# A hybrid decoder block: projections in another order, a top-k over 50 pairs, rows normed in steps, loads issued elsewhere

## The chip, the cores and the metric

The kernel runs on one core of a Trainium2 chip, whose engines work in parallel, each through its own queue in order: TensorE (PE in the profile; PEld is its weight load), VectorE (DVE), ScalarE (ACT), GpSimd (POOL) and SyncE (SP), which only starts transfers. ACT's and POOL's queues start transfers too. The metric is the device time of one execution in microseconds (us).

## What is computed

One decoder block over 528 tokens (16 meta tokens and 512) of 2048 channels: an RMS norm, one wide projection, a convolution module and a gated linear attention (GLA) side by side, their gated sum projected back, and then a channel mixer (PEER) in which each token picks experts by a product key.

```python
proj = rmsnorm(h, norm1_g) @ w_in        # split into a_conv, q, k, v, r, a_low, g_merge
y_conv = conv_module(a_conv)             # h*sigmoid, 31 taps, layer norm, silu, @ w_conv_out
y_gla = gla(q, k, v, r, a_low)           # chunked, rms norm, * silu(r), @ w_gla_out
gates = sigmoid(g_merge)
h = h + (gates[:, :D] * y_conv + gates[:, D:] * y_gla) @ w_out
xn = rmsnorm(h, norm2_g); q = xn @ peer_wq           # 8 heads of 2 x 128
s1 = q[..., :128] @ k1; s2 = q[..., 128:] @ k2       # 128 keys each
v1, i1 = top_k(s1, 16); v2, i2 = top_k(s2, 16)
cand = v1[:, None] + v2[None, :]                     # 16 x 16 pairs
top_s, pos = top_k(cand, 16); idx = i1[pos//16]*128 + i2[pos%16]
w = softmax(top_s) * gelu(U[idx] @ xn)               # 16384 experts
out = rmsnorm(h + w @ V[idx], normf_g)[16:]
```

## The kernel before

Activations stand with channels on the 128 partitions and tokens along the row. Each fp32 product is made of three matmuls over a number split into a high and a low part (x = xh + xl, weights whi + wlo: xl by whi, xh by whi, xh by wlo), 48 matmuls for 16 tiles of 128 channels. `_weights` (line 59) loads a weight tile in two halves through SP's queue, ACT casts each half to `whi` (L69), and DVE or POOL subtracts to `wlo` (L72): `g.lopool` names the halves that POOL takes. `whi` and `wlo` have three buffers each, so one and a half projections can be prepared ahead. Loop order is written by hand; a list scheduler with a cost model of its own then sets the order on each engine from it, and `high_priority` and `issue_after` shift its choice.

The stages: `_norm1`; `_phase_a` with 16 convolution tiles, each two projections of 528 columns (`_conv`) and after it one of the 48 gate projections of 512 columns (`_gates`, which stores sigmoid or silu rows to `rgd`), then the GLA heads with four gate projections, then the other 28 gate projections, under which the convolution's layer norm statistics and normed rows (`_conv_stats`, `_conv_norm`) are made; `_mixers_out`, first `wco` (convolution) and then `wgo` (GLA, whose rows o*r are made at its start); `_residual`; `_select`, 16 projections `wq` with `_scores` (a top-16 of 128 scores, four blocks of tokens) and after each second one `_head_select` (top-16 of 256 pairs, two `_pick`s of the indices), and beside them `_dense_row`, which norms the rows that the experts' matmuls read (`dh`, `dl`).

The 160 gathered tokens (of 512) get their experts' rows by indirect DMA (`rows`) and DVE; the 352 dense ones get a matmul with all 16384 experts: 128 up tiles `_up_tile` (`pu`, gelu rows `gel`, the first 64 stored to `hlag`) and 16 groups of down products (`_down_quarter`, `pv`). The first `NPRE` up tiles run while DVE still selects; their `wlo` are POOL's. `_w_piece` multiplies four gelu rows by the gate matrix `gt` and splits them (`wh`, `wl`). In the last group `_Final` adds the residual `hx` to the sums `yT` before each quarter and finishes the gathered tokens.

Of the kernel before, what the change touches and what calls it, by code (L numbers as in the profile page):

```python
# [6 lines left out]
F32 = mybir.dt.float32  # L7
# [22 lines left out]
EPS = 1e-6  # L30
TB0 = 128
# [9 lines left out]
NINT = 16  # L41
NPRE = 8
# [83 lines left out]
def _norm1(g, sp):  # L126
# [3 lines left out]
    with g.tc.tile_pool(name="n1", bufs=1, side="right") as tp:  # L130
        ss = [tp.tile([P, L], F32, name="ss", bufs=2) for _ in range(2)]
        xe = []
        with g.tc.high_priority(offset=100000):
            for c in range(KT // 2):
                xe.append(tp.tile([P, 2, L], F32, name="xe", bufs=8))
                nc.sync.dma_start(xe[c], a["xe"][:, 2 * c:2 * c + 2])
                if c == 0:
                    g.w0 = _weights(g, a["wp"][16])
        for k in range(KT):
# [51 lines left out]
def _conv_stats(g, sp, csum, mu):  # L191
    nc = g.nc
    ps = _colsum(g, csum)
    nc.vector.tensor_scalar(mu, ps, 1.0 / D, None, op0=OP.mult)
    vs = sp.tile([P, SEQ], F32, name="vs")
    for ct in range(KT):
        x = sp.tile([P, SEQ], F32, tag="lnx", name="lnx", bufs=2)
        nc.scalar.dma_start(x, g.convd[ct])
        nc.vector.tensor_tensor(x, x, mu, op=OP.subtract)
        q = vs if ct == 0 else sp.tile([P, SEQ], F32, tag="lnq", name="lnq", bufs=1)  # L200
        nc.scalar.activation(q, x, AF.Square)
        if ct:
            nc.vector.tensor_tensor(vs, vs, q, op=OP.add)
    return vs
# [249 lines left out]
def _phase_a(g):  # L454
    nc, tc, a = g.nc, g.tc, g.a
    with ExitStack() as es:
# [8 lines left out]
        with tc.tile_pool(name="gla", bufs=1, side="right") as gp:  # L465
# [30 lines left out]
        g.ch = g.ap.tile([P, KT, SEQ], F32R, tag="ah", name="ch")  # L496
        g.cl = g.ap.tile([P, KT, SEQ], F32R, tag="al", name="cl")
        lp = es.enter_context(tc.tile_pool(name="ln", bufs=1))
        mu = lp.tile([P, SEQ], F32, name="mu")
        rstd = lp.tile([P, SEQ], F32, name="rstd")  # L500
        vs = _conv_stats(g, lp, csum, mu)
        for ct in range(NINT + 4, 48):
            if ct == NINT + 14:
                _rsqrt(g, lp, rstd, [(slice(0, SEQ), _colsum(g, vs))], SEQ, 1.0 / D)
                _conv_norm(g, lp, mu, rstd, g.ch, g.cl)
            _gates(g, cp, ct)
# [7 lines left out]
def _mixers_out(g):  # L514
    nc, tc, a = g.nc, g.tc, g.a
    with tc.tile_pool(name="evb", bufs=1) as ep, tc.tile_pool(name="actB", bufs=1) as bp:
        oh = bp.tile([P, KT, SEQ], F32R, name="oh")
        ol = bp.tile([P, KT, SEQ], F32R, name="ol")
        for ct in range(KT):
            o = ep.tile([P, SEQ], F32, name="bo", bufs=2)  # L520
            nc.scalar.dma_start(o, g.od[ct])
            r = ep.tile([P, SEQ], F32, name="br", bufs=2)
            nc.scalar.dma_start(r, g.rgd[ct])
# [674 lines left out]
```

## Time and profile before

| what | us |
|---|---|
| median of 3 runs (lowest, highest) | 4354.86 (4352.84, 4356.57) |
| the profiled execution | 4358.66 |
| its span in the trace | 4356.9 |
| PE busy | 4234.4 (97%) |
| DVE busy | 3218.8 (74%) |
| ACT busy, POOL busy | 1429.6, 884.4 |

The span reaches from the first to the last instruction; 1.8 us of the profiled execution lie around it. An engine's busy time counts pipelined instructions once, so a busy PE can still be a slow one: the clock column of the views tells at which of its two levels (1.2 or 2.4 GHz) it ran. In a wait, the name behind the arrow is what came last.

### The profile page before, as it was taken

To read this page: it belongs to the slowest core of one execution; us is meant where nothing else is said; L and a number is where in the kernel's file an instruction comes from. 1 tells how busy PE (TensorE), PEld (TensorE's weight loads), DVE (VectorE), ACT (ScalarE), POOL (GpSimd) and SP (SyncE) were. 2 spreads that over 40 slices of the span, in tenths; PEclk is the share of its full clock that TensorE was granted. 3 is DMA by queue.
4 is the path that set the end of the run, shared out by engine and by line. 5 is a ranking of instruction groups with operands and counts; after the bars stand their busy time and mean duration, and the time that the engine had idled before them with its cause. 6 is when DMAs were issued, how large, how long until landed. Compare 5 with 4: busy or idle time off the path is not lost.

```text
span 4356.9 us, 63349 instructions
## 1 busy us (share of the span) xinstructions
PE 4234.4 (97%) x25360; PEld 3937.4 (90%) x25360; DVE 3218.8 (74%) x4578; ACT 1429.6 (33%) x1844; POOL 884.4 (20%) x664
## 2 busy tenths in 40 slices
PE   8999999999999999999889999989999999999998
PEld 8888889999888888887679999989999999999998
DVE  8999985655554433334999888678888888888876
ACT  4222223333445222223223333333333333333323
POOL 2222210000000000003342222233332222222230
PEclk9999999999999999999999999999999999999999
DMA  4333322222344554443327888899999999999984
GB/s 157 102 102 102 102 97 74 81 80 75 112 152 145 187 173 142 140 139 106 97 95 273 321 330 328 321 335 334 356 349 339 347 341 356 343 352 346 349 329 149
DMA packets 235433, 943.15 MB, mean 216 GB/s; under 512 B 27264, under 2 KB 40256, under 8 KB 194176
## 3 DMA queue, kind: packets, MB, share of 16 engines
q1 hardware_dynamic: 126944, 458.94, 30.9%
q0 software_dynamic: 65216, 399.54, 24.4%
q10 hardware_dynamic: 42976, 80.62, 5.2%
q8 instruction: 198, 3.24, 0.3%
q14 instruction: 99, 0.81, 0.1%
HBM read 870.83 MB, written 68.16 MB: 216 GB/s over the span
## 4 chain that ended last, share of the span: by engine, by line
PE 79%; DVE 15%; issue 3%; DMA 2%; ACT 1%; POOL 0%; DVEq 0%; SPq 0%; ACTq 0%; POOLq 0%
PE mm L91 10%; PE mm L93 10%; PE mm L89 10%; DVE cacc L176 8%; PE pu L89 7%; PE pu L93 7%; PE pu L91 7%; PE pv L898 7%; PE pv L896 7%; PE pv L897 7%; DVE wlo L72 2%; PE pg L814 2%; PE ps L404 1%; PE ps L367 1%; PE ps L410 0%
## 5 line engine op out<-in xcount | busy, mean ns | idle before, releaser
L69 ACT CAST whi<-raw 128x1024 fp32r<-128x1024 f32 x866 | 904.4, 1047 | 2174.7 <-PE mm L91 650.9
L72 DVE TENSOR_TENSOR wlo<-raw,whi 128x1024 fp32r<-128x1024 f32 (+1 forms) x773 | 976.5, 1265 | 568.1 <-ACT whi L69 566.8
L93 PE MATMUL mm<-xh,wlo 128*128 128x264 f32 (+2 forms) x2720 | 727.7, 322 | 20.8 <-POOL wlo L72 19.7
L89 PE MATMUL mm<-xl,whi 128*128 128x264 f32 (+2 forms) x2720 | 735.0, 324 | 11.0 <-DVE xl L143 11.0
L91 PE MATMUL mm<-xh,whi 128*128 128x264 f32 (+2 forms) x2720 | 726.8, 322 | 0.0
L898 PE MATMUL pv<-wh,wlo 128*128 128x352 f32 x2048 | 663.5, 324 | 21.9 <-DVE wlo L72 21.9
L89 PE MATMUL pu<-dl,whi 128*128 128x352 f32 x2048 | 666.4, 325 | 12.4 <-ACT whi L69 12.4
L93 PE MATMUL pu<-dh,wlo 128*128 128x352 f32 x2048 | 658.4, 321 | 10.9 <-DVE wlo L72 8.7
L896 PE MATMUL pv<-wl,whi 128*128 128x352 f32 x2048 | 663.2, 324 | 2.9 <-ACT whi L69 1.5
L897 PE MATMUL pv<-wh,whi 128*128 128x352 f32 x2048 | 662.5, 323 | 0.0
L91 PE MATMUL pu<-dh,whi 128*128 128x352 f32 x2048 | 657.8, 321 | 0.0
L93 PEld LDWEIGHTS mm<-xh,wlo 128*128 128x128 f32 (+1 forms) x2720 | 450.1, 188 | 66.4 <-POOL wlo L72 25.3
L89 PEld LDWEIGHTS mm<-xl,whi 128*128 128x128 f32 (+1 forms) x2720 | 452.2, 188 | 57.7 <-DVE xl L143 11.7
L91 PEld LDWEIGHTS mm<-xh,whi 128*128 128x128 f32 (+1 forms) x2720 | 449.9, 187 | 42.9 <-issue 4.2
L176 DVE SCALAR_TENSOR_TENSOR cacc<-hg,cw,cacc 128x512 f32<-128x512 f32 x480 | 413.3, 861 | 15.2
L898 PEld LDWEIGHTS pv<-wh,wlo 128*128 128x128 f32 x2048 | 388.0, 189 | 24.2 <-DVE wlo L72 24.2
L89 PEld LDWEIGHTS pu<-dl,whi 128*128 128x128 f32 x2048 | 385.8, 188 | 12.7 <-ACT whi L69 12.7
L93 PEld LDWEIGHTS pu<-dh,wlo 128*128 128x128 f32 x2048 | 385.4, 188 | 12.5 <-DVE wlo L72 9.6
L896 PEld LDWEIGHTS pv<-wl,whi 128*128 128x128 f32 x2048 | 387.9, 189 | 3.6 <-ACT whi L69 1.8
L897 PEld LDWEIGHTS pv<-wh,whi 128*128 128x128 f32 x2048 | 387.8, 189 | 0.1
L91 PEld LDWEIGHTS pu<-dh,whi 128*128 128x128 f32 x2048 | 386.6, 189 | 0.0
L737 POOL DMA_INDIRECT rows<-un,eidx x128 | 192.2, 1501 | 560.1 <-DVE rows L758 544.1
(306 smaller groups left out, 5599.6 us busy)
## 6 DMA issues: line engine op xcount, KB each, us to landing
raw<-ut SPq DMA_DIRECT2D x256, 512.0 KB
raw<-vt SPq DMA_DIRECT2D x256, 512.0 KB
raw<-wp SPq DMA_DIRECT2D x224, 512.0 KB
gd<-stage ACTq DMA_DIRECT2D x44, 512.0 KB
gt<-gd POOLq DMA_DIRECT2D x32, 704.0 KB
raw<-wco SPq DMA_DIRECT2D x32, 512.0 KB
raw<-wgo SPq DMA_DIRECT2D x32, 512.0 KB
raw<-wo SPq DMA_DIRECT2D x32, 512.0 KB
```

The costliest lines, as they stand in the source:

```text
L69: nc.scalar.copy(hi, raw)
L72: g.last = eng.tensor_tensor(lo, raw, _bf(hi), op=OP.subtract).ins
L89: nc.tensor.matmul(ps, wh, xl[:, k, cs], start=k == 0, stop=False)
L91: nc.tensor.matmul(ps, wh, xh[:, k, cs], start=False, stop=False)
L93: nc.tensor.matmul(ps, wl, xh[:, k, cs], start=False, stop=k == KT - 1)
L176: nc.vector.scalar_tensor_tensor(acc, hg[:, w:w + SEQ], cw[:, w:w + 1], acc, op0=OP.mult, op1=OP.add)
L367: nc.tensor.matmul(ps[:, x * P:(x + 1) * P], e[:, 0, i:i + P], e[:, 1, i:i + P], start=d == 0, stop=d == 1)
L737: nc.gpsimd.indirect_dma_start(out=rows[:, :], out_offset=None, in_=src, in_offset=bass.IndirectOffsetOnAxis(ap=idx[:, col:col + 1].bitcas ...
L814: nc.tensor.matmul(ps[:, j * P:(j + 1) * P], b8[:, t], ag[:, t], start=True, stop=True)
L896: nc.tensor.matmul(o, hi[:, c:c + P], wl[:, j], start=first, stop=False)
L897: nc.tensor.matmul(o, hi[:, c:c + P], wh[:, j], start=False, stop=False)
L898: nc.tensor.matmul(o, lo[:, c:c + P], wh[:, j], start=False, stop=last)
```

## The change

Two gate projections follow each convolution tile instead of one (32 of 48). Of the 12 gate projections that are left behind GLA, each has pieces of o*r and of the statistics after it; `wgo` now runs first, the convolution's rows are normed under it, and `wco` follows. `_head_select` forms the 50 pairs (i, j) with (i+1)(j+1) <= 16, which hold the top 16, in place of 256; it is called after every third score step and, for four heads, between up tiles, and needs some ten small operations more to turn a place among the 50 into two indices. `_dense_row` has three steps, in different turns of the loop: the load, the scaling on POOL (was DVE), and a split on ACT and DVE. The first 10 up tiles (was 8) come before the second part. `_w_load` issues a piece's loads two quarters before its use, from one `hlag` tensor for each four rows. In the last group the residual is added after a quarter, two loads ahead, and the gathered tokens' work is spread over three quarters. The first input tile is loaded in two halves.

```diff
-NINT = 16
-NPRE = 8
+NINT = 32
+NPRE = 10
...
                 for ct in range(KT):
                     g.lopool = (1,) if ct else ()
                     _conv(g, sp, ct, csum)
-                    if ct < NINT:
-                        _gates(g, cp, ct)
+                    for i in range(2 * ct, 2 * ct + 2):
+                        _gates(g, cp, i)
...
+        todo = _gla_rows(g, lp, g.oh, g.ol) + _conv_stats(g, lp, csum, g.mu)
+        n = 48 - NINT - 4
+        for i in range(n):
+            _gates(g, cp, NINT + 4 + i)
+            for f in todo[i * 2 * KT // n:(i + 1) * 2 * KT // n]:
+                f()
+        _rsqrt(g, lp, g.rstd, [(slice(0, SEQ), _colsum(g, g.vs))], SEQ, 1.0 / D)
...
+    h = sp.tile([P, TD], F32, tag="gel", name="dnh", bufs=6)
+
+    def load():
+        nc.gpsimd.dma_start(h, g.hd[ct, :, TG:])
+
+    def scale():
+        nc.gpsimd.tensor_tensor(h, h, g.rs2[:, TG:], op=OP.mult)
+
+    def split():
+        g2 = g.vec[:, V_N2 + ct:V_N2 + ct + 1]
+        nc.scalar.activation(g.dh[:, ct], h, AF.Copy, scale=g2)
+        nc.vector.scalar_tensor_tensor(g.dl[:, ct], h, g2, _bf(g.dh[:, ct]), op0=OP.mult, op1=OP.subtract)
...
+    cand = sp.tile([P, 4, n], F32, name="tkc", bufs=1)
+    for j in range(8):
+        w = NCAND[j]
+        nc.vector.tensor_tensor(cand[:, :, CAND0[j]:CAND0[j] + w], V[:, 1, :, :w], V[:, 0, :, j:j + 1].to_broadcast([P, 4, w]), op=OP.add)
+    nc.vector.tensor_tensor(cand[:, :, CAND0[8]:], V[:, 0, :, 8:], V[:, 1, :, 0:1].to_broadcast([P, 4, 8]), op=OP.add)
...
+        if i % 3 == 1 and i > 1:
+            _head_select(g, sp, *g.heads.pop(0))
...
+            if 2 <= i < 12:
+                for step in (2, 1, 0):
+                    for ct in (2 * i - 4 - 2 * step, 2 * i - 3 - 2 * step):
...
     for u in range(NPRE):
         _up_tile(g, u, True)
+        if u % 2 == 0 and g.heads:
+            _head_select(g, sp, *g.heads.pop(0))
...
+                if q % 2 == 0 and grp + 1 < NGRP:
+                    ld = _w_load(g, 2 * (grp + 1) + q // 2, grp + 1 < LAGG)
                 los = _down_quarter(g, grp, q, ws)
...
-        g.hlag = dp.tile([8 * LAGG, P, TD], F32, name="hlag")
+        g.hlag = [dp.tile([4, P, TD], F32, name=f"hlag{i}") for i in range(2 * LAGG)]
```

How the instructions stand then, at three places, all in POOL's queue, which is waited for by PE or by DVE. In the convolution stage, one period of it, before (`hg` is the gated input, `rgd` the store of a gate row):

```order
L164 MEMSET hg 128x14
L72 TENSOR_TENSOR wlo<-raw,whi 128x1024 x2
L449 DMA rgd<-gev 128x512
L72 TENSOR_TENSOR wlo<-raw,whi 128x1024
L169 TENSOR_TENSOR hg<-hg,rs_87 128x528
```

and in the changed kernel:

```order
L174 TENSOR_TENSOR hg<-hg,rs_102 128x528
L74 TENSOR_TENSOR wlo<-raw,whi 128x1024 x2
L476 DMA rgd<-gev 128x512
L74 TENSOR_TENSOR wlo<-raw,whi 128x1024
L476 DMA rgd<-gev 128x512
L74 TENSOR_TENSOR wlo<-raw,whi 128x1024
L169 MEMSET hg 128x14
```

A second store and a fourth low half stand in a period, which now holds two gate projections beside the convolution's own two; the clearing of `hg` comes behind the low halves.

In the selection, beside the projections `wq`, one turn and a half before (`dnh` is a dense row, `hd` the stored residual):

```order
L580 DMA dnh<-hd 128x352
L72 TENSOR_TENSOR wlo<-raw,whi 128x1024 x2
L580 DMA dnh<-hd 128x352
L72 TENSOR_TENSOR wlo<-raw,whi 128x1024 x3
L580 DMA dnh<-hd 128x352 x2
L72 TENSOR_TENSOR wlo<-raw,whi 128x1024 x2
```

and in the changed kernel:

```order
L604 DMA dnh<-hd 128x352 x2
L74 TENSOR_TENSOR wlo<-raw,whi 128x1024 x2
L607 TENSOR_TENSOR dnh<-dnh,rs_14822 128x352 x2
L604 DMA dnh<-hd 128x352 x2
L74 TENSOR_TENSOR wlo<-raw,whi 128x1024 x2
L607 TENSOR_TENSOR dnh<-dnh,rs_14822 128x352 x2
```

The two loads are followed by the two low halves of a projection, as before, and then by two scalings of the rows that were loaded a turn earlier.

In the first groups of down products, where gelu rows come back from `hlag`, before:

```order
L869 DMA gel_24632<-hlag 128x352
L869 DMA gel_24637<-hlag 128x352
L869 DMA gel_24642<-hlag 128x352
L869 DMA gel_24932<-hlag 128x352
L737 DMA rows<-un,eidx 128x2048
L863 DMA gt<-gd 128x11x128
L869 DMA gel_24937<-hlag 128x352
L869 DMA gel_24942<-hlag 128x352
L869 DMA gel_24947<-hlag 128x352
L869 DMA gel_25237<-hlag 128x352
```

and in the changed kernel:

```order
L927 DMA gel_24438<-hlag_67 128x352
L927 DMA gel_24440<-hlag_67 128x352
L927 DMA gel_24442<-hlag_67 128x352
L927 DMA gel_24741<-hlag_68 128x352
L797 DMA rows<-un,eidx 128x2048
L923 DMA gt<-gd 128x11x128
L927 DMA gel_24743<-hlag_68 128x352
L927 DMA gel_24745<-hlag_68 128x352
L927 DMA gel_24747<-hlag_68 128x352
L927 DMA gel_25048<-hlag_69 128x352
```

Loads, gathers and gate matrices stand in the same order; only the tensor that is read has a number. On DVE, where the heads were put off in the code, the last row of head h (counted from 0) had about 2h + 2.7 score steps ahead of it and now has 2h + 3, for all heads but the last two.

## Rows read from the trace of the kernel before

**Rows 1.** Windows by stage; columns: stretch, us, engines, clock, DMA share, GB/s.
```profile
45.00:565.00 520.00, 499.20 (x3412) 462.75 (x3411) 502.61 (x571) 141.56 (x144) 138.91 (x86) 1.00 0.32 102
565.00:2005.00 1440.00, 1439.49 (x7768) 1224.21 (x7767) 702.30 (x1096) 472.66 (x577) 51.89 (x76) 1.00 0.38 124
2005.00:2345.00 340.00, 294.23 (x1460) 255.49 (x1459) 305.74 (x988) 103.29 (x180) 139.50 (x70) 0.93 0.36 119
...
2830.00:3200.00 370.00, 353.09 (x2165) 350.76 (x2164) 308.61 (x383) 121.93 (x160) 123.81 (x122) 0.98 0.93 341
3200.00:4225.00 1025.00, 1024.85 (x6443) 1024.56 (x6443) 878.22 (x788) 336.45 (x404) 290.91 (x216) 1.00 0.93 347
4225.00:4357.00 132.00, 108.46 (x665) 106.15 (x663) 86.58 (x103) 47.55 (x85) 19.49 (x12) 0.92 0.50 170
sum 4357.00, PE 4234.45 PEld 3937.37 DVE 3218.77 ACT 1429.57 POOL 884.36; mean PE 529.31 PEld 492.17 DVE 402.35 ACT 178.70 POOL 110.54
```

**Rows 2.** Sum over the six half-clock stretches of 2037.9 to 2321.3 us.
```profile
sum 44.50, PE 26.95 PEld 23.42 DVE 37.62 ACT 10.28 POOL 25.09; mean PE 4.49 PEld 3.90 DVE 6.27 ACT 1.71 POOL 4.18
```

**Rows 3.** One convolution period: windows row, then groups of VectorE and GpSimd.
```profile
232.94:269.29 36.35, 34.88 (x241) 32.41 (x241) 35.32 (x41) 9.82 (x10) 9.62 (x7) 1.00 0.33 102
...
L72 DVE TENSOR_TENSOR wlo<-raw,whi 128x1024 fp32r<-128x1024 f32 x3 | 5.8, 1949 | 0.0
...
L72 POOL TENSOR_TENSOR wlo<-raw,whi 128x1024 fp32r<-128x1024 f32 x4 | 10.1, 2546 | 0.3 <-ACT whi L69 0.2
```

**Rows 4.** Timeline of VectorE, then TensorE, in the selection: start, us.
```profile
2029.92 0.55 DVE L587 MAX8 tkv<-tkS 128x8 f32<-128x128 f32 x2 [14.02 <-ACT tkS L629]
...
2301.68 0.68 DVE L668 TENSOR_TENSOR gate<-gate,tkm 128x512 f32<-128x512 f32 x1
...
2315.93 0.73 DVE L732 COPY gatex<-gate 32x32 f32<-32x32 f32 x4
...
2317.97 0.66 PE L93 MATMUL pu<-dh,wlo 128*128 128x352 f32 x1 [6.28 <-DVE wlo L72]
```

**Rows 5.** TensorE's waits, 2005 to 2345 us; columns: total us, times, longest us.
```profile
PE pu L89 <- ACT whi L69: 12.4, 1, 12.4
...
PE ps L221 <- DVE rx L715: 3.2, 1, 3.2
```

**Rows 6.** Waits of the other engines, 2005 to 2345 us.
```profile
ACT dh L510 <- DVE dnh L581: 97.4, 14, 20.2
...
POOL dnh L580 <- DVE dl L511: 44.6, 6, 13.5
ACT tkS L629 <- DVE tkx L589: 29.7, 3, 18.1
```

**Rows 7.** VectorE groups, 2005 to 2340 us: count, busy us, mean ns, idle.
```profile
L646 DVE TENSOR_TENSOR tkc<-tkv 128x256 f32<-128x256 f32 x32 | 31.4, 982 | 0.0
...
L591 DVE FIND_INDEX8 tki<-tkv,tkx 128x8 uint32<-128x128 f32 x64 | 18.0, 281 | 0.0
...
L591 DVE FIND_INDEX8 tkp<-gate,tkc 128x8 uint32<-128x256 f32 x32 | 13.3, 416 | 0.0
...
L581 DVE SCALAR_TENSOR_TENSOR dnh<-dnh,vec,rs 128x352 f32<-128x352 f32 x16 | 11.4, 718 | 5.6 <-DMA dnh<-hd 5.6
...
L650 DVE TENSOR_SCALAR tku<-tkp 128x64 uint32<-128x64 uint32 x8 | 9.1, 1142 | 0.0
...
L651 DVE TENSOR_SCALAR tku<-tkp 128x64 uint32<-128x64 uint32 x8 | 3.7, 464 | 0.0
```

**Rows 8.** TensorE's waits, 2830 to 3200 us, and GpSimd's timeline.
```profile
PE pv L898 <- DVE wlo L72: 15.4, 7, 5.3
...
2842.63 0.54 POOL L869 DMA_DIRECT2D gel<-hlag  x1 [8.21 <-DMA hlag<-gel]
```

**Rows 9.** VectorE's waits, 4225 to 4357 us.
```profile
DVE yT L1044 <- DMA hx<-hd: 8.2, 1, 8.2
```

More of the change, by code (lines that the diff above doesn't have):

```diff
@@ L30 @@
 EPS = 1e-6
+NCAND = [TOPK // (j + 1) for j in range(TOPK)]
+CAND0 = [sum(NCAND[:j]) for j in range(TOPK + 1)]
 TB0 = 128
@@ L194, in _conv_stats, with piece, f, _gla_rows @@
     nc.vector.tensor_scalar(mu, ps, 1.0 / D, None, op0=OP.mult)
[L195 to L204, printed above, removed]
+    vs = g.vs = sp.tile([P, SEQ], F32, name="vs")
+    def piece(ct):
+        def f():
+            x = sp.tile([P, SEQ], F32, tag="lnx", name="lnx", bufs=2)
+            nc.scalar.dma_start(x, g.convd[ct])
+            nc.vector.tensor_tensor(x, x, mu, op=OP.subtract)
+            q = vs if ct == 0 else sp.tile([P, SEQ], F32, tag="lnq", name="lnq", bufs=1)
+            nc.scalar.activation(q, x, AF.Square)
+            if ct:
+                nc.vector.tensor_tensor(vs, vs, q, op=OP.add)
+        return f
+    return [piece(ct) for ct in range(KT)]
+def _gla_rows(g, sp, oh, ol):
+    nc = g.nc
+    def piece(ct):
+        def f():
+            o = sp.tile([P, SEQ], F32, name="bo", bufs=2)
+            nc.scalar.dma_start(o, g.od[ct])
+            r = sp.tile([P, SEQ], F32, name="br", bufs=2)
+            nc.scalar.dma_start(r, g.rgd[ct])
+            nc.vector.tensor_tensor(o, o, r, op=OP.mult)
+            _split_store(g, o, oh[:, ct], ol[:, ct])
+        return f
+    return [piece(ct) for ct in range(KT)]
 def _conv_norm(g, sp, mu, rstd, oh, ol):
@@ L680, in _select @@
     qT = None
+    rows = []
+    g.heads = []
     g.rc = sp.tile([P, 4], F32, name="rc")
@@ L863, in _w_piece @@
         nc.gpsimd.dma_start(gt.rearrange("p b j t -> p b (j t)"), g.gd[:, :, 4 * p:4 * p + 4].rearrange("b p j t -> p b (j t)"))
+        ges = []
+        for j in range(4 if lag else 0):
+            ge = g.up.tile([P, TD], F32, tag="gel", name="gel2", bufs=g.gels)
+            nc.gpsimd.dma_start(ge, g.hlag[p][j])
+            ges.append(ge)
+    return gt, ges
+def _w_piece(g, ld, ges=None):
+    nc = g.nc
+    gt, lagged = ld
+    with g.tc.high_priority(offset=g.pri):
         wh = g.vp.tile([P, 4, TD], F32R, name="wh", bufs=3)
         wl = g.vp.tile([P, 4, TD], F32R, name="wl", bufs=3)
[L866 to L871 removed]
+        for j, ge in enumerate(ges or lagged):
             nc.vector.tensor_tensor(ge.rearrange("p (b t) -> p b t", t=TB), ge.rearrange("p (b t) -> p b t", t=TB), gt[:, :, j], op=OP.mult)
@@ L946, in _peer @@
             if u == nlag - 2:
-                ws = [_w_piece(g, p, None) for p in range(2)]
+                ws = [_w_piece(g, _w_load(g, p, True)) for p in range(2)]
+        fin = None
         for grp in range(NGRP):
@@ L1038, in sums, with residual, after @@
         return self.g.pu.tile([P, 512], F32, tag="pu", name="ss")
-    def before(self, q):
+    def residual(self, q):
         g = self.g
         y = g.yT[:, 4 * q:4 * q + 4]
-        g.nc.vector.tensor_tensor(y, y, self.hx, op=OP.add)
-        if q < 3:
-            self.load(q + 1)
-    def after(self, q):
+        g.nc.vector.tensor_tensor(y, y, self.hx[q], op=OP.add)
+        if q < 2:
+            self.hx.append(self.load(q + 2))
+    def after(self, q, los):
         g, nc = self.g, self.g.nc
+        with g.tc.issue_after(los[-1]):
+            if q < 3:
+                self.residual(q)
+                self.gathered(q)
+            if q == 2:
+                self.residual(3)
         for ct in range(4 * q, 4 * q + 4):
```

222 lines of the change are left out of this document (108 added, 114 removed).

## The prediction

> **What bounds it now.** I read the windows by stage first, for the engine that is full and for where it is not. TensorE is busy for 4234.45 of 4357 us [rows 1]. The stretches 565 to 2005 and 3200 to 4225 have under 1 us of idle in them: there only less matmul work would save time, and the change takes no matmul out. So the whole of the possible gain lies in the 122.5 us of idle (4357 - 4234.45), plus what a clock under 1.00 costs. By stage, idle is the stretch less PE's busy time: convolution 20.8, selection 45.8, first down groups 16.9, last group 23.5; the two stretches not shown keep the remaining 15. The clock column says that PE ran partly at the half level (1.2 GHz) in three stages: the six stretches in the selection sum to 44.50 us with 26.95 of PE busy, which at full clock would have taken half as long: 13.5 lost [rows 2]. They lie behind the long waits, so a wait costs more than itself.
>
> The sum goes against the profiled execution, 4358.66, which is 3.8 above the median of the runs shown.
>
> **The change part by part.**
>
> *First input tile.* Half of a tile stands ahead of the first weights in SP's queue where a whole one stood. No row of mine prices it; it lies between nothing and about 1 us, and I take 0.5, since the other tiles follow in the same order and the norm needs them all.
>
> *Convolution, second gate.* One period took 36.35 us, PE 34.88 of it and DVE 35.32 [rows 3]: VectorE sets this stage, and PE's 1.5 us of idle a period is the 20.8 of the stage. A second gate projection adds 48 matmuls to PE. A 352-column matmul takes 1024.85/6443 = 0.159 us [rows 1], so a 512-column one 0.231 and the projection 11.1: PE then needs 46.0 a period. VectorE's additions: one low half more (1.95, the mean of three), the multiplication that evicts a gate row (512 columns, 0.68 for such an operation in [rows 4]), and, at worst, being held once more for a whole low half of GpSimd (2.55): 35.3 + 5.2 = 40.5. GpSimd has four low halves, 10.2. So PE is the longest by over 5 us and sets the period. I take 23, above the 20.8 for the clock and the refilling after a wait, which the two stretches not shown also hold; bounds 21 and 26.
>
> *Fewer gates behind GLA.* 32 pieces of rows and statistics now fall to 12 projections of 11.1 us, 2.7 to each. Each has two VectorE operations of 512 columns, 0.68 each: 3.6, with two low halves (3.9) and the eviction (0.7) that makes 8.2 of 11.1. Before, 565 to 2005 had DVE at 702.30 of 1440 and PE without a wait [rows 1]. I cost it, and `wgo` before `wco`, at nothing; the cover is the one and a half prepared projections, and if that goes, what is late is a low half, some 2 us for each time.
>
> *Selection and first up tiles.* Here most of the time lies: 44.2 of idle that I ascribe to the waits on other engines (the matmul sums' own gaps aside) and the 13.5, together 57.7. The longest wait, 12.4, is for ACT's high half, with `rx` another 3.2 [rows 5]. Why ACT was late is in the other engines' waits: ACT stood 97.4 us, 14 times, for VectorE's scaling of a dense row, and 29.7 for the top-16's buffer; GpSimd stood 44.6 for the row's buffer [rows 6]. VectorE is a queue in order with a long selection in it, and the dense row joins ACT and GpSimd to it. The change cuts this: GpSimd scales, and each step comes a turn after the one before. GpSimd's price is 2.546 x 352/1024 = 0.88 us a row, 14 for 16, 2 a turn beside two low halves.
>
> Then VectorE's own chain must end in time. It ran from the first score operation at 2029.92 to the spread gates at 2315.93 + 0.73 = 2316.7: 287 us, after which PE resumed at 2317.97, having waited 6.28 for a low half [rows 4]. Its terms: FIND_INDEX8 takes 281 ns for 128 columns and 416 for 256 [rows 7], so 1.05 ns a column, 199 for 50; I give the five operations of each of the 32 top-16s that saving, 160 x 0.217 = 35. The pair sums go from 32 of 982 ns to 72 small ones. Their rows are not in the trace; the nearest are 0.18 (a quarter of the 0.73 of four copies) and 0.46 (L651): 13 to 33, and I take 20, since most hold 4 to 64 numbers as the copies do. That saves 11 (-2 to 18). Seven small operations more a head, 56, cost 10 to 26; I take 15. The scaling leaves with 11.4 and the 5.6 that it waited for its load. Chain: 287 - 35 - 11 + 15 - 17 = 239, end at 2269 (2247 to 2290).
>
> When does PE need it? VectorE takes over the low halves after ten up tiles instead of eight, 2 x 48 x 0.159 = 15.3 us later. Without its 57.7 of waits PE would be there at 2318 - 57.7 + 15.3 = 2275. On ACT the softmax's exponential stands ahead of the gelu rows of the last two tiles, so it must come 15 earlier, at about 2260; the subtraction ahead of it stood 15 before the chain's end (2301.68), which gives 2254. Both are just in time. I leave the `rx` wait and its clock (5) and 3 for small misses: gain 50, bounds 20 and 53.
>
> *First down groups.* PE waits 15.4 in seven times for the low half of a down weight, the longest 5.3; GpSimd, whose queue also loads gelu rows, stood 8.21 for a store to `hlag` [rows 8], because one tensor's loads wait for all its stores. With a tensor for each four rows that goes. The loads stand in the same order as before (the third pair of rows of the order), and with five buffers a load still waits for its buffer; VectorE, whose queue has the multiplications on those rows ahead of low halves, then waits as before. So I take only what follows the 8.21: the 5.3 and some 1.5 before it, and 2 of the clock: 9. Bounds: nothing, and 24, the whole 16.9 and the 0.02 of clock on 370 us.
>
> *Last group.* VectorE stood 8.2 for the residual [rows 9]. Adding it after a quarter, loaded ahead, takes that away; of the clock's 0.08 on 132 us I give this wait 3: 11. New is that the gathered tokens' transposes share two `pu` buffers with VectorE full: PE then queues behind an eviction, about 3. Gain 8, bounds 0 and 11. What follows the last matmul stays.
>
> Sum: 0.5 + 23 + 50 + 9 + 8 = 90.5, so 4268.2 for the profiled execution and **4264** as a median.
>
> **A rule against it.** Two operations of one shape on VectorE, two lines apart, take 1142 and 464 ns [rows 7], and its low half 1.95 us in the mean [rows 3]: something outside holds it at times, and GpSimd was at work on 139.5 of those 340 us [rows 1]. The Trainium skill, SBUF — State Buffer, "Who interferes with whom", says that a VectorE instruction with two SBUF inputs is blocked by a GpSimd instruction that reads SBUF, for the whole instruction. The trace agrees with it in kind. The Trainium skill, Perfetto Trace Analysis, "Optimizing Scalar/DVE Operations", draws from it that offloading between those two might not help.
>
> **The rivals.**
>
> *Moved work gains nothing.* The 14 us of scaling on GpSimd hold VectorE for as long, and the 17 are not saved: the chain ends at 2286, 11 too late, and with its clock costs some 14: 4278. If the 128 added or split operations (72 and 56) also cost 0.46, the chain grows by another 13 + 11: 2310, and 4302. For it: the 1142 above. Against it: GpSimd is busy under half of the stage. In the middle 4289.
>
> *All waits go.* ACT, free of the dense rows, also prepares weights so early that the `rx` wait vanishes, and loads issued ahead do bring the gelu rows in time: 1 + 26 + 57.7 + 24 + 11 = 120, 4235; I put it at 4240. Against it: the same order of loads.
>
> *Convolution's waits return.* Four low halves on GpSimd hold VectorE through a longer period, and it stays the bound: the 23 is lost, 4287. It needs over 5 us a period beyond my worst case.
>
> *Slower.* The small operations of the selection on VectorE, 72 and 88 of them, each wait for half a GpSimd low half (1.27) before their 0.2. Against the 0.27 that I took, 1.2 more for 160 of them makes the chain 192 longer; it ends at 2461, PE waits 186 for it, and the time is 4450. It turns slower than before where the chain ends 90 us after 2275, so from 0.27 + 96/160 = 0.87 us an operation. Against it: with GpSimd busy for 41% of the stage the mean wait would be about 0.5.
>
> *It doesn't do what it says.* The heads, put off in the code, move by a third of a score step on VectorE, and the loads ahead stand where they stood; both are counted at nothing above. For the whole to be within 0.2% (8.7 us, about what a measurement of this kernel can tell from no change) the convolution and the dense rows would have to fail together.
>
> **Numbers.** Forecast 4264 with its own range 4250 to 4284: 0.55. Moved work gains nothing: 0.20. All waits go: 0.13. Convolution's waits return: 0.05. Slower: 0.05. No change: 0.02. The range of 4238 to 4304 leaves out the last two, a third of the case of all waits, and a little of the others. Faster 0.93, within 0.2% 0.02, slower 0.05.
>
> **What would show it.** Right: the convolution's period near 46 us with PE full in it; no wait of ACT for a dense row on VectorE and no 12.4 for the high half; the gates spread by about 2269 and before PE asks; no 8.21 in GpSimd's queue, with most of the small waits for low halves of down weights left; no wait of VectorE for `hx`. Wrong: VectorE's small operations well over 0.3 us in the mean, GpSimd's scaling standing in a low half's way so that PE waits for `wlo` of `wq`, new waits of PE for a piece's loads among gates 36 to 47, or a new wait in the last group.

## The result, and the profile after

The changed kernel took 4305.2 us (4304.41 to 4310.87, four runs) against 4355.72 for the kernel before in the same comparison: a ratio of 0.9886, interval 0.9874 to 0.9898, 50 us faster. 4264 was forecast, and the range ended at 4304. The profiled execution spans 4302.6 us, 54.3 less than before; the prediction's sum was 90.5.

Windows by stage of the kernel after (columns as in [rows 1]):

```profile
45.00:780.00 735.00, 735.00 (x4642) 665.07 (x4641) 591.90 (x686) 183.93 (x194) 192.32 (x122) 1.00 0.34 110
1360.00:1410.00 50.00, 42.58 (x173) 32.77 (x172) 33.35 (x47) 19.56 (x29) 2.17 (x4) 0.97 0.69 224
1990.00:2330.00 340.00, 313.30 (x1656) 279.90 (x1655) 296.59 (x1073) 117.78 (x197) 169.19 (x92) 0.96 0.40 130
2785.00:3200.00 415.00, 399.80 (x2465) 396.30 (x2464) 350.20 (x438) 137.61 (x181) 145.23 (x141) 0.98 0.94 344
4180.00:4303.00 123.00, 105.63 (x657) 103.46 (x655) 88.00 (x103) 47.39 (x91) 18.21 (x12) 0.93 0.53 174
```

TensorE's idle in a stretch is the stretch less its busy time, the first of the engines' columns. The convolution is without idle now (20.8 in [rows 1]). The stretch around 1385, under the gate projections behind GLA, has 7.4, where the kernel before had next to none (0.5 over 565 to 2005). The selection's idle fell from 45.8 to 26.7, that of the first down groups only from 16.9 to 15.2.

What each stage gave is best read by the start of the same matmul in both traces: the colsum (the sum over the channels of the residual's squares, which ends the residual's stage and starts the selection's), the first down product, the 2600th, and the end of the last matmul. In the table that follows, every run of this study stands in these pieces of its profiled execution, in us; the ratio is to the kernel before in the same comparison.

| kernel | to the colsum | from there to the first down product | 2600 down products | to the last matmul | median of runs, ratio to before |
|---|---|---|---|---|---|
| before | 2009.0 | 819.7 | 439.6 | 1073.2 | 4355.72 |
| after | 1995.4 | 790.2 | 436.9 | 1064.4 | 4305.2, 0.9886 |
| gained | 13.6 | 29.5 | 2.7 | 8.8 | |
| predicted | 23.5 | 50 | 9 | 8 | |
| e1_gel | 1996.6 | 801.7 | 447.1 | 1062.8 | 4324.0, 0.9927 |
| e2_bo | 1985.9 | 787.7 | 442.9 | 1064.4 | 4295.1, 0.9859 |
| e3_heads | 1994.4 | 789.6 | 433.6 | 1064.3 | 4298.5, 0.9867 |
| e4_dvscale | 1996.1 | 784.6 | 437.4 | 1062.8 | 4299.0, 0.9877 |
| e5_late | 1996.0 | 781.8 | 433.1 | 1062.8 | 4294.9, 0.9863 |
| e6_conv | 2011.4 | 819.4 | 433.1 | 1073.7 | 4356.1, 1.0005 |
| e7_last | 1999.3 | 802.0 | 424.1 | 1062.8 | 4305.2, 0.9883 |
| e8_best | 1984.5 | 810.8 | 428.5 | 1064.4 | 4303.6, 0.9878 |
| e9_pairs | 1998.2 | 807.6 | 441.0 | 1064.4 | 4326.6, 0.9933 |
| e10_three | 1982.6 | 794.7 | 439.1 | 1062.8 | 4294.5, 0.9856 |
| e11_dense | 1984.3 | 793.4 | 440.4 | 1066.0 | 4297.3, 0.9865 |
| e12_two | 1983.0 | 785.1 | 435.3 | 1062.8 | 4284.2, 0.9842 |
| e13_fourteen | 1985.0 | 774.7 | 437.4 | 1064.4 | 4276.5, 0.9822 |
| e14_twelve | 1997.0 | 787.5 | 434.9 | 1064.4 | 4298.0, 0.9869 |

Each ratio has an interval of about 0.0017 to either side (0.0012 for the changed kernel, 0.001 for e6_conv). That is some 7 us, so runs that stand under 10 us apart can hardly be told from each other by their times. The pieces help only so far: the first one spread from 1994.4 to 1999.3 over the eight kernels that share its code (after, e1, e3, e4, e5, e7, e9, e14). A difference of 5 us in one piece of one trace is therefore not a gain shown; the waits in the traces have to bear it out.

In the selection, the waits of TensorE in the kernel after; the first was to go (12.4 in [rows 5]), the second is new at that length:

```profile
PE pu L91 <- ACT whi L71: 10.0, 1, 10.0
PE ps L657 <- ACT qT L642: 8.3, 1, 8.3
PE ps L248 <- DVE rx L775: 3.2, 1, 3.2
```

and those of ACT there:

```profile
ACT tkS L661 <- DVE tkx L621: 49.0, 5, 13.9
...
ACT dh L611 <- POOL dnh L607: 27.3, 14, 3.8
```

The 97.4 of [rows 6] for a dense row became 27.3, but the copies of scores, whose wait was 29.7 there, wait 49.0 for VectorE's top-16. TensorE's 8.3 and 10.0, both where the last scores meet the first up tiles, are the `qT` and the weight cast that stand behind such a copy in ACT's queue (ACT's timeline):

```profile
2193.03 0.37 ACT L661 ACTIVATE tkS<-ps,rc 128x128 f32<-128x128 f32 x1 [13.87 <-DVE tkx L621]
...
2195.93 0.61 ACT L642 COPY qT<-mm 128x512 f32<-128x512 f32 x1
...
2218.89 1.14 ACT L661 ACTIVATE tkS<-ps,rc 128x128 f32<-128x128 f32 x4 [12.78 <-DVE tkx L621]
2219.90 2.01 ACT L71 CAST whi<-raw 128x1024 fp32r<-128x1024 f32 x2
```

### The profile page after: what moved, and what is told of

It reads as the page before. It is cut to its first block, busy times and chain, and to the rows that moved or that the text cites. A ratio compares the mean times of both kernels' runs of the same rounds, so it can differ in the third digit from the quotient of the medians.

```text
span 4302.6 us, 63437 instructions
## 1 busy us (share of the span) xinstructions
PE 4219.7 (98%) x25360; PEld 3929.1 (91%) x25360; DVE 3175.5 (74%) x4639; ACT 1395.9 (32%) x1818; POOL 954.1 (22%) x699
## 4 chain that ended last, share of the span: by engine, by line
PE 88%; DVE 7%; DMA 3%; issue 1%; ACT 1%; POOL 0%; ACTq 0%; DVEq 0%; SPq 0%; POOLq 0%
PE mm L95 13%; PE mm L93 13%; PE mm L91 13%; PE pv L966 7%; PE pv L964 7%; PE pv L965 7%; PE pu L91 7%; PE pu L95 7%; PE pu L93 7%; PE pg L874 2%; DVE wlo L74 1%; DMA bo<-od 1%; DMA lnx<-convd 1%; PE ps L431 1%; PE ps L394 1%
## 5 line engine op out<-in xcount | busy, mean ns | idle before, releaser
L74 DVE TENSOR_TENSOR wlo<-raw,whi 128x1024 fp32r<-128x1024 f32 x754 | 923.8, 1227 | 495.0 <-ACT whi L71 493.2
L95 PEld LDWEIGHTS mm<-xh,wlo 128*128 128x128 f32 (+1 forms) x2720 | 449.9, 188 | 50.6 <-DVE wlo L74 10.8
L181 DVE SCALAR_TENSOR_TENSOR cacc<-hg,cw,cacc 128x512 f32<-128x512 f32 x480 | 453.1, 944 | 15.3
L74 POOL TENSOR_TENSOR wlo<-raw,whi 128x1024 fp32r<-128x1024 f32 x112 | 280.7, 2509 | 318.1 <-ACT whi L71 297.5
```

What stands on the lines that cost most here:

```text
L74: g.last = eng.tensor_tensor(lo, raw, _bf(hi), op=OP.subtract).ins
L95: nc.tensor.matmul(ps, wl, xh[:, k, cs], start=False, stop=k == KT - 1)
L181: nc.vector.scalar_tensor_tensor(acc, hg[:, w:w + SEQ], cw[:, w:w + 1], acc, op0=OP.mult, op1=OP.add)
```

## The experiments

**Behind GLA.** The kernel after in the stretch with the twelve gate projections: the waits of TensorE and VectorE from 1360 to 1410, and then VectorE's timeline:

```profile
PE mm L95 <- DVE wlo L74: 7.4, 5, 2.6
```

```profile
DVE bo L227 <- DMA bo<-od: 16.3, 6, 4.0
```

```profile
1394.66 0.69 DVE L227 TENSOR_TENSOR bo<-bo,br 128x512 f32<-128x512 f32 x1 [3.97 <-DMA bo<-od]
1395.27 1.22 DVE L74 TENSOR_TENSOR wlo<-raw,whi 128x1024 fp32r<-128x1024 f32 x1
```

The low half that TensorE wants starts as soon as the product on the row of o, which had to wait for its load, is made. e2_bo gives the row a third buffer:

```diff
-            o = sp.tile([P, SEQ], F32, name="bo", bufs=2)
+            o = sp.tile([P, SEQ], F32, name="bo", bufs=3)
```

> The changed kernel with three buffers in place of two for the GLA rows bo that are loaded behind gates 36 to 47. Theory: VectorE stands 22.8 us there for the load bo<-od, because a buffer comes free only when the row before is split and the load takes 4.7 us; low halves queue behind it, and TensorE loses 7.2 us and 1.7 of clock between 1369 and 1409 us. With a third buffer the load starts a row earlier: most of the 9 us goes, about 4297. Rival: the loads stand too late in ACT's queue, behind casts that wait for VectorE, whatever buffer is free; then nothing changes, 4305.

TensorE has no wait there any more:

```profile
1350.00:1400.00 50.00, 50.00 (x218) 40.53 (x217) 35.23 (x49) 21.61 (x31) 2.71 (x5) 1.00 0.75 249
```

The first piece became 9.5 us shorter and the time 4295. The theory holds. Five later runs carry the third buffer too: the first piece is 1984.2 in the mean of these six traces and 1996.6 in the mean of the eight without it, so the two buffers cost 9.5 to 12. Whether the convolution's own step was right is tested by e6_conv, the kernel before with the second gate alone:

```diff
-NINT = 16
+NINT = 32
...
-                    if ct < NINT:
-                        _gates(g, cp, ct)
+                    for i in range(2 * ct, 2 * ct + 2):
+                        _gates(g, cp, i)
```

> The kernel before with one part of the change alone: two gate projections after each convolution tile, 12 behind GLA with the convolution's statistics and rows under them as before. My step of the prediction: 20.8 of idle and a little of the clock, 21 to 23 us, and no wait behind GLA as the GLA rows are not loaded there: 4355 to 4333. Rival: in the period of 46 us, as the changed kernel has it, something else holds TensorE back, or the statistics under 12 projections wait as the GLA rows did in the changed kernel, 9 us: 4342.

Nothing was gained: 4356.1, ratio 1.0005 (0.9995 to 1.0015). The convolution is full in it too; the windows row of the stretch in which `wco` begins, and TensorE's waits around it, say where the time went:

```profile
1450.00:1550.00 100.00, 83.50 (x323) 63.28 (x324) 57.31 (x79) 38.01 (x51) 3.25 (x6) 0.93 0.59 195
```

```profile
PE mm L89 <- DVE cl L216: 13.5, 8, 5.2
```

16.5 of idle and a clock of 0.93: the convolution's normed rows come late for the first products. In the code they stand behind the tenth of the projections after GLA (`if ct == NINT + 14`, which this edit leaves as it is), so that two projections lie behind them in place of eighteen. The last sum of squares, the colsum over them, the first rows and the first product on them, from VectorE's and TensorE's timelines:

```profile
1375.47 0.69 DVE L203 TENSOR_TENSOR vs<-vs,lnq 128x512 f32<-128x512 f32 x1 [0.76 <-ACT lnq L201]
...
1422.52 1.02 PE L187 MATMUL ps<-vs,ones 128*128 128x512 f32 x2
...
1438.01 1.29 DVE L216 TENSOR_TENSOR cl<-lnx,ch 128x512 fp32r<-128x512 f32 x2 [1.23 <-ACT ch L215]
...
1445.62 0.39 PE L89 MATMUL mm<-cl,whi 128*128 128x512 f32 x1
```

The first row is made 7.6 us ahead of the product that reads it; in the kernel before it was 185 (1285.8 and 1471.3). My theory for this run was wrong, and the result is worse than its rival. The 16 projections that moved had covered that work. What the run does not show is that the new order behind GLA is the only cure: the squares were summed 46 us before the colsum came in its place, and a kernel with the rows that much earlier was not run. In the changed kernel `wgo` stands between, and the rows are normed under it.

**The selection.** e4_dvscale takes the scaling of the dense rows back from GpSimd:

```diff
-        nc.gpsimd.tensor_tensor(h, h, g.rs2[:, TG:], op=OP.mult)
+        nc.vector.tensor_tensor(h, h, g.rs2[:, TG:], op=OP.mult)
```

> The changed kernel with the scaling of the dense rows on VectorE again, one turn after the load as now. Theory (VectorE's own work is the bound in the score loop): 16 scalings of about 0.7 us more make its chain 11 us longer, and TensorE waits that much more: 4313 to 4318. Rival (the scalings on GpSimd hold VectorE as long as they take, so that moving them gained nothing): VectorE's copies and multiplications get shorter by as much as it takes over, and the time is 4302 to 4308.

The piece became 5.6 us shorter, and VectorE's chain, counted from the colsum to the spread gates, 290.2 in place of 294.9 (before 307.7): both about as much as such pieces vary by. What VectorE did in the chain is clearer. Windows over the chain (VectorE's is the third busy time), the kernel after and then e4_dvscale:

```profile
1995.43:2290.32 294.89, 271.72 (x1396) 240.04 (x1395) 265.22 (x1032) 100.23 (x172) 155.81 (x83) 0.96 0.34 108
```

```profile
1996.09:2286.30 290.21, 272.31 (x1397) 239.36 (x1396) 254.49 (x1048) 99.09 (x172) 141.70 (x67) 0.98 0.34 110
```

Groups of VectorE in the kernel after:

```profile
L631 DVE TENSOR_TENSOR pk<-iota,tkq 128x1024 f32<-128x1024 f32 x16 | 27.7, 1734 | 0.3
...
L612 DVE SCALAR_TENSOR_TENSOR dl<-dnh,vec,dh 128x352 fp32r<-128x352 f32 x16 | 16.3, 1032 | 6.1 <-ACT dh L611 6.1
...
L705 DVE CAST eidx<-tkg 128x16 int32<-128x16 f32 x8 | 10.7, 1342 | 0.1
```

and in e4_dvscale:

```profile
L631 DVE TENSOR_TENSOR pk<-iota,tkq 128x1024 f32<-128x1024 f32 x16 | 21.5, 1341 | 0.2
...
L612 DVE SCALAR_TENSOR_TENSOR dl<-dnh,vec,dh 128x352 fp32r<-128x352 f32 x16 | 11.8, 745 | 2.7 <-ACT dh L611 2.7
...
L607 DVE TENSOR_TENSOR dnh<-dnh,rs 128x352 f32<-128x352 f32 x16 | 8.3, 521 | 23.1 <-DMA dnh<-hd 23.1
...
L705 DVE CAST eidx<-tkg 128x16 int32<-128x16 f32 x8 | 5.7, 712 | 0.1
```

VectorE took 8.3 us of scaling over and was yet at work for 10.7 us less: its other operations, unchanged in number and shape, took 19.0 less beside a GpSimd that no longer had the 15.5 of scaling. A comparison over 1024 columns became 6.2 us shorter, the rows' split 4.5 and a cast of 16 columns 5.0. The rival holds, that of the prediction too, and by more than either said: the work that was moved cost VectorE more than it took off. That it gained nothing is as the rule of the Trainium skill has it (Perfetto Trace Analysis, "Optimizing Scalar/DVE Operations").

TensorE's waits in e4_dvscale show why the time moved so little:

```profile
PE ps L248 <- DVE rx L775: 8.5, 1, 8.5
PE mm L95 <- POOL wlo L74: 3.3, 4, 1.3
PE pu L91 <- ACT whi L71: 2.2, 1, 2.2
...
PE ps L657 <- ACT qT L642: 1.9, 2, 1.4
```

The two long waits, 8.3 and 10.0, are all but gone, though no head stands elsewhere; ACT's wait for the top-16 fell from 49.0 to 11.7. Against that, `rx` comes 5.3 later, because VectorE now stands 18.3 us at the start of the stage for the load of the first dense row, and 3.3 of waits for GpSimd's low halves are new.

e9_pairs undoes the 50 pairs:

```diff
-    cand = sp.tile([P, 4, n], F32, name="tkc", bufs=1)
...
+        cand = sp.tile([P, TOPK, TOPK], F32, name="tkc", bufs=1)
```

> The changed kernel with one part undone: the head's selection among 256 pairs again, with its few and larger operations (and one row buffer less). By the terms of my prediction VectorE's chain becomes longer by 35 + 11 - 15 = 31 us, and since it sets TensorE's waits there, the time by 20 to 31: 4325 to 4336. Rival (the small operations are held by GpSimd so often that the 50 pairs gain little): chain longer by under 10, time 4305 to 4315.

The chain became 313.3, 18.4 longer, the piece 17.4, and the time 4326.6. The pairs are worth 18 of the 31 that the terms gave. (The scheduler also set the heads of this run up to three score steps later, so the number is not of the pairs alone.)

e3_heads was to put the heads off, by the code alone, and to run 14 up tiles ahead of the second part:

```diff
-NPRE = 10
+NPRE = 14
...
-        if i % 3 == 1 and i > 1:
+        if i % 5 == 1 and i > 1:
...
```

> The changed kernel with two heads in place of four selected beside the projections (after every fifth score step), the other six between up tiles, of which 14 in place of 10 come before the second part; one gelu buffer less there. Theory: VectorE falls behind in the score loop (a head of some 17 us and three score steps of 6.4 and the dense rows need more than the 35 us of three projections), ACT's copies of the scores wait for it (49.0 us for tkx) with the casts of weights queued behind them, and so TensorE waits 8.35 and 10.0. With a head for each five steps VectorE keeps up: both waits and their 4.5 of clock go, and those at the hand-over too: 4305 to about 4283. Rival: what holds VectorE is GpSimd, each of whose operations blocks it; then the chain is as long wherever the heads stand, TensorE waits at the end of it for what it did not wait for before, and the time is 4300 to 4310.

It tests nothing of the heads: the scheduler set them at the places that they have in the changed kernel, and the waits stayed, 8.37 and 9.35. It does show that four more up tiles alone gain nothing (789.6 for 790.2, with one gelu buffer less). e5_late ties them to the score step ahead of them, with 12 up tiles:

```diff
-NPRE = 10
+NPRE = 12
...
-            _head_select(g, sp, *g.heads.pop(0))
+            with tc.issue_after(g.tkl):
+                _head_select(g, sp, *g.heads.pop(0))
...
```

> The changed kernel with its heads held on VectorE behind the score step that stands ahead of them in the code (in the run before this, and in the changed kernel, the scheduler had them at the same places as each other: heads after 3, 5, 7, ... score steps; now after 4.4, 7.4, 10.4, 13.4 and four after the last), and 12 up tiles in place of 10 before the second part. Theory (VectorE falls behind in the score loop because a head stands in every two steps; ACT's copies of scores, with casts of weights behind them, wait for its top-16): with three steps to a head TensorE's waits of 8.35 and 10.0 and 4.5 of clock go, and the two more tiles cover the end of the chain: 4305 to about 4283. Rival (whatever the order, VectorE is held by GpSimd and ends as late, and TensorE then waits at the hand-over or for gelu rows behind the exponential): 4298 to 4308.

TensorE's waits in e5_late:

```profile
PE pu L91 <- ACT whi L71: 7.4, 1, 7.4
PE pu L95 <- DVE wlo L74: 4.8, 1, 4.8
PE ps L248 <- DVE rx L776: 3.2, 1, 3.2
PE pu L95 <- POOL wlo L74: 2.1, 1, 2.1
...
PE ps L657 <- ACT qT L642: 0.5, 1, 0.5
```

Both long waits are gone, and the 7.4, 4.8 and 2.1 stand at the chain's end (2287 to 2300 us): 8.4 us gained of 22. Each theory was half right. e14_twelve, with the two more tiles alone (`NPRE = 12`), parts the two edits:

> The changed kernel with 12 in place of 10 up tiles before the second part and nothing else, to part the two edits of the run e5_late. Theory (its 8 us came from the heads' places): the waits of 8.35 and 10.0 stay, only the 1.7 at the hand-over goes: 4302 to 4305. Rival (they came from the two tiles): about 4295, with the two long waits gone or shorter.

In it 8.3 and 9.9 stay, and the piece is 2.7 shorter: that the two waits went in e5_late is due to the heads' places. The time, 4298.0, lies between theory and rival and doesn't decide.

e10_three joins the edits of e2_bo, e5_late and e4_dvscale:

> The changed kernel with three edits of the runs before together: the third buffer for bo (it gave 9.4 us by the 1527.3 against 1536.7 at the 8500th projection matmul), the heads put off with 12 up tiles (8 us by the first down product), the scaling on VectorE (5 us there). Theory (VectorE's chain from the first score to the spread gates is what TensorE waits for, in the loop or at its end, and the scaling on GpSimd lengthened it by more than it took off): the last two act on one chain and add up: 4305 - 9.4 - 8 - 5 = 4283, down to 4278 with the clock. Rival (each of the two only moves the same wait, so that the second finds nothing left): 4288 to 4292.

4294.5, above both forecasts, and the piece 794.7 against 781.8 in e5_late. With the heads late, the scaling on VectorE gains nothing and seems to cost: VectorE stood 35.4 us for the loads of dense rows. e11_dense moves the rows two turns later:

```diff
-            if 2 <= i < 12:
+            if 4 <= i < 14:
...
-                    for ct in (2 * i - 4 - 2 * step, 2 * i - 3 - 2 * step):
+                    for ct in (2 * i - 8 - 2 * step, 2 * i - 7 - 2 * step):
```

> The three edits of the run e10_three, with the dense rows' three steps two turns later. In that run VectorE, which scales them, stood 35.4 us for their loads, 18.5 of it at the start, where the residual had only just been stored, and the transposes of the norm's row came 5 us later for it. Theory (VectorE's own chain is what TensorE waits for, and here it was lengthened by loads that were not there yet): the chain, 285.4 us there, becomes 20 to 25 shorter, the waits of TensorE at its end (5.8, 2.05, 3.5 and 8 of clock) go, with the 5 at the start: 4294 to 4274 or 4279. Rival (TensorE's waits are set by something else, ACT or GpSimd's low halves): 4288 to 4295.

That theory fell: the chain, which I had expected 20 to 25 shorter, stayed at 314.5 from the colsum, and VectorE now stood 30.8 for scores and 14.3 for the loads. What sets it there is not VectorE alone, and I can't say what it is. Without the scaling on VectorE, e12_two:

> The changed kernel with the third buffer for bo and the heads put off, and the scaling left on GpSimd. If the gains of the two single runs (9.4 and 8 us) lie in different stages, as I hold, they add up: 4305 - 17 = 4288, with what the first groups vary by (their 2600 first down products took 433 to 443 us in runs that had the same order there) 4283 to 4292. Rival (the two overlap, as the run with three edits, 4294, would have it): 4294.

4284.2: the two gains add up in the time, as theory had it. By the pieces it is less clear: 12.4 in the first, 5.1 in the selection (8.4 in e5_late) and 3.2 in the two stages that no edit touched. What is left in its selection shows in ACT's timeline:

```profile
2274.65 0.63 ACT L727 ACTIVATE gate<-gate 128x512 f32<-128x512 f32 x1 [14.42 <-DVE gate L726]
```

The exponential stands in ACT's queue ahead of weight casts and waits for VectorE's subtraction. With `NPRE = 14` (e13_fourteen) it stands two tiles further back:

> The run e12_two with 14 up tiles in place of 12 ahead of the second part. There ACT stood 14.4 us at the softmax's exponential for VectorE's subtraction, with the casts of weights behind it, and TensorE 7.4 and 2.1 for it, 4.1 at the hand-over, and some 7 of clock. Theory (the chain of VectorE is too long only for where the program wants its end): two tiles, 15.4 us, cover it; those 20 go and the time is 4284 to about 4266. Rival (the end of the chain moves with the tiles, or the gate matrices, with 47 in place of 49 tiles to be built under, become the next wait): 4278 to 4286.

TensorE's waits in e13_fourteen:

```profile
PE pu L95 <- DVE wlo L74: 4.8, 1, 4.8
PE ps L248 <- DVE rx L776: 3.2, 1, 3.2
PE pu L95 <- POOL wlo L74: 2.4, 1, 2.4
```

The piece is 774.7, 45.0 less than before, and the time 4276.5, 0.9822 (0.9806 to 0.9839): the best of the study, 77 us under the kernel before in its comparison and 29 under the changed one. The exponential's wait fell from 14.4 to 7.3, and the 7.4 that TensorE waited behind it is gone. The chain's end moved back too (311.2 from the colsum, 305.4 in e12_two), so the rival holds in part: where VectorE takes the low halves over from GpSimd, TensorE still waits, 4.8 (4.1 in e12_two).

**The first down groups.** The waits of GpSimd for rows of `hlag`, in the kernel before (2760 to 3250 us):

```profile
POOL gel L869 <- DMA hlag<-gel: 17.7, 2, 9.5
```

and in the kernel after:

```profile
POOL gel L927 <- DVE wl L539: 39.3, 19, 5.2
...
POOL gel L927 <- DMA hlag<-gel: 17.4, 2, 9.4
```

The wait that the separate tensors were to remove, 8.21 in [rows 8], is there still, as 8.0 (17.4 less the 9.4), and so is the other one. e1_gel gives loads and up tiles buffers of their own:

```diff
-        ge = g.up.tile([P, TD], F32, tag="gel", name="gel", bufs=g.gels)
+        own = g.gels == GEL and (lag or u % 5 in (1, 3))
+        ge = g.up.tile([P, TD], F32, tag="gelu" if own else "gel", name="gel", bufs=2 if own else 3 if g.gels == GEL else g.gels)
...
-            ge = g.up.tile([P, TD], F32, tag="gel", name="gel2", bufs=g.gels)
+            ge = g.up.tile([P, TD], F32, tag="gel", name="gel2", bufs=3)
```

> The changed kernel with the gelu rows that an up tile writes and those that come back from hlag in buffers of two tags (2 and 3 in place of 5 shared). Theory: GpSimd's load that waits 8.0 us for the store hlag<-gel (2799.61 us) waits for its buffer, which an up tile's row still holds until it is stored, and not for the tensor in DRAM, since there are separate tensors now; so with own buffers GpSimd's waits of 9.4 and 8.0 for hlag<-gel go, and TensorE's 5.6 at 2807 us with them: 7 to 10 us with the clock, about 4297. Rival: the wait is on the tensor after all, or on the multiplications that free the buffers; then the 5.6 stays and the time is 4305, or up to 4312 since three buffers for loads are fewer than five.

In e1_gel no wait for `hlag<-gel` is left, so it was for the buffer, which an up tile's row holds until it is stored, and not for the tensor:

```profile
POOL gel L928 <- DVE wl L539: 79.6, 31, 5.9
```

But this wait, for the buffers that the multiplications free, doubled, and the time is 4324. Of the profiled execution's loss 10.2 lies in the groups, where three buffers are the likely cause, and 11.5 ahead of them: there VectorE stood 13.4 us for the first gate matrix. e7_last leaves the five to the loads, the last three up tiles going into a buffer that is free then:

```diff
...
+        own = vp.tile([P, 4, TD], F32, tag="wl", name="own", bufs=3)
         for u in range(nlag - 3, nlag):
-            _up_tile(g, u, True)
+            _up_tile(g, u, True, own[:, u - nlag + 3])
```

> The changed kernel with the gelu rows of the three last stored up tiles (61 to 63) in a buffer of another tag that is free at that time. Theory: the loads of the first groups wait 9.4 and 8.0 us for hlag<-gel because these three rows hold gelu buffers until they are stored; with five buffers for the loads those waits go and with them TensorE's 5.6 and 1.2 at 2807 us and 2.6 of clock: 4305 to 4296. Rival (with the store gone from the way, the multiplications on VectorE are next and free the buffers as late): 4303 to 4308.

The wait for the store is gone here too, and the groups took 424.1, 12.8 less. The piece ahead of them took 11.8 more. VectorE's waits from 2760 to 2800 us in e7_last, and TensorE's from 2330 to 2900:

```profile
DVE gel L941 <- DMA gel<-hlag: 16.7, 3, 12.7
```

```profile
PE pu L95 <- DVE wlo L74: 6.9, 3, 5.7
```

The stall only moved ahead of the first down product: VectorE stands 12.7 us for the first rows, with low halves behind it. Time unchanged, 4305.2. e8_best, the edits of e10_three with this one, shows the same trade:

> The same three edits, and the gelu rows of up tiles 61 to 63 in a buffer of their own, which by itself gave nothing (the first groups became 12.7 us shorter, the stretch ahead of them 9.5 longer, where VectorE then stood for the first loads with low halves behind). Theory: the same again, within 3 us of the run without it. Rival: with VectorE ahead in the selection the first loads come earlier, only the gain of the first groups is left, and it is 8 to 12 us faster than the run without it.

4303.6, slower than e10_three, so neither theory holds: the stretch ahead lost 16.1 against e10_three, and the groups gained 10.6. From 2760 to 2800 us TensorE was idle for 9.8 in it, at a granted clock of 0.79 (6.5 and 0.91 in e7_last). Why the stretch loses more than they gain is not settled.

## Why the prediction was wrong

Its direction, its bound and two of the terms were right. The gains of the pieces add up to what the profiled execution gained, and of the 36 that are missing 10 are in the first piece, 20 in the selection and 6 in the first down groups. The period of the convolution came out as worked out, TensorE full, VectorE below it: 45.7 us from one clearing of `hg` to the next, for 46.0 (a stretch of 46 us of the kernel after):

```profile
191.00:237.00 46.00, 46.00 (x291) 41.75 (x290) 37.28 (x43) 12.79 (x13) 12.71 (x9) 1.00 0.35 109
```

With the third buffer the first piece gains 24.8 (mean of six traces) for the 23.5 of the forecast. The last group gave 8.8 for 8; the wait of [rows 9] for `hx` is gone. In the start the first matmul comes 0.56 earlier, for 0.5. Three steps failed, and a fourth was wrong in its mechanism.

1. "I cost it, and `wgo` before `wco`, at nothing": the twelve gates behind GLA cost 9.5 to 12 (e2_bo and the runs that carry its edit). The sum of VectorE's work, 8.2 of 11.1, was not wrong (33.35 of the 50 us around 1385); what was left out is that its queue stands for a row with two buffers, while the low half behind it could start. I named only the prepared projections as cover. The 16 projections that left had been another, for the normed rows: with these left in their place, the loss is the whole gain (e6_conv); in the changed kernel, with `wgo` ahead of `wco`, no product waits for them.

2. "Chain: 287 - 35 - 11 + 15 - 17 = 239": it was 274.0, and from the colsum 12.8 shorter, not 48. Summed over VectorE's operations in the chain, before and after, the top-16s of pairs gave 33 for 35 and the pair sums 12 for 11. The small operations of the heads cost 25 for 15 (25.5 to 50.6), and two groups that I had left as they were became longer: those of 1024 columns in the picks by 12.5 (62.2 to 74.7) and the rows' splits, in a new form, by 7. So the failed terms are the 15 and the -17. The scaling's 11.4 left VectorE, but I let the other operations keep the times that they had beside a GpSimd with less to do; e4_dvscale took 19.0 off them by taking the scaling back. That was the rival with 0.20, "moved work gains nothing"; its upper end, 4302, is near the result, but partly by luck: its price leaves out the first step, the third and the down groups.

3. "When does PE need it?" was answered at the chain's end alone. In the score loop VectorE is late as well, and the copies of scores tie ACT to it: the third row of [rows 6] showed this wait, 29.7, and I let it go with the dense rows. It became 49.0 and took 18.3 of TensorE's time and 4.5 of clock (two stretches at the half level, 9.03 us busy). Two edits take the waits away, each alone: the heads later (e5_late) and the scaling off GpSimd (e4_dvscale). So a good part of this step is again the work that was moved. That the end is a place in the program, and not only a length, e13_fourteen shows: the selection then gave 45.0, near the 50.

The 9 for the first down groups was 2.7, which is within what this stage varies by in one trace. The step "because one tensor's loads wait for all its stores" was wrong in its mechanism (e1_gel), so the change did nothing to this wait; and 9 was too much even for its removal (e7_last gave nothing on balance). The statement that the loads stood in the same order was right.

What stays open: what holds the chain in e11_dense, whether the second gate alone would gain with the normed rows made earlier, and how much of the small differences between runs (5 us) belongs to the edits.

## What to carry to other kernels

Before filling an engine's gaps with work from elsewhere, ask what that work was hiding there: the second gate alone, with the normed rows left in their place, gained nothing. Before moving an operation to GpSimd, count what it does there to VectorE's other operations. Follow a late engine through every queue that waits for it, at each turn of a loop and not only where its work must be finished. And look in the scheduled order whether an edit of the code moved anything before pricing it.

## What the runs showed of the hardware

A cast of 128x16 on VectorE took 157 ns in the mean in the kernel before, 1342 in the kernel after and 712 with the scaling off GpSimd. I had put such operations at 0.18 to 0.46; some small ones of the head stayed at 0.16 to 0.24, others took 0.4 to 1.3 (the key's multiplication 1029). Single operations of the kernel after show why: two of these casts, and GpSimd beside the first:

```profile
2168.32 2.32 DVE L705 CAST eidx<-tkg 128x16 int32<-128x16 f32 x1
...
2260.92 0.16 DVE L705 CAST eidx<-tkg 128x16 int32<-128x16 f32 x1
```

```profile
2165.79 4.82 POOL L74 TENSOR_TENSOR wlo<-raw,whi 128x1024 fp32r<-128x1024 f32 x2 [9.52 <-ACT whi L71]
```

The first cast ends 0.03 us after GpSimd's second low half; beside the other one GpSimd has no operation. Of the eight casts, four took 2.28 to 2.39 us and each ended 0.03 after a low half, one took 0.91 and ended 0.03 after a scaling, and three took 0.16 to 0.20. So the time that VectorE is held stands inside the operation's own recorded time and not as a wait. The 1142 ns that the prediction found is the same: one of the eight operations took 5.85 us, beside three low halves. The rule as the prediction gives it is on operations with two inputs in SBUF; these have one tensor as input and were held as well. The top-16's operations were not: FIND_INDEX8 over 128 columns took 276 to 294 ns in all 128 cases of the kernel after. The mean of a small operation says little where another engine is at work; its place beside GpSimd's does.

The 2600 first down products took 433 to 443 us in the eleven kernels that have the changed kernel's code there (all in the table but before, e6_conv, e1_gel, e7_last and e8_best), and 439.6 and 433.1 in before and e6_conv, which share theirs; so a gain of under 10 us in that stretch can't be read from one trace.
